# A PEER decoder block: token groups (0,1,2)+(3) become (0,1)+(2,3), block 0 gathers its U rows and adds its weights to a DRAM table

## The chip, the cores and the metric

The kernel runs on one core of a Trainium2 chip. A time is the device time of one execution in microseconds (us). Engine names are those of the profile: PE is TensorE (PEld its weight loads), DVE is VectorE, ACT is ScalarE, POOL is GpSimd, SP issues most DMAs.

## The reference

One decoder block over 512 tokens of width 1024 plus 16 meta tokens. First a mixer: stick-breaking attention (8 heads of 64) beside gated linear attention (4 heads), one input projection and one output projection. Then the PEER layer, which takes most of the time:

```
q = (t @ w_peer_q)                      # per token 8 heads, two halves of 64
s1, s2 = q1 . sub_keys1, q2 . sub_keys2 # 128 scores each
16 best of each, 16 best of the 256 sums -> 16 experts (of 128*128) and softmax gates per head
act = gelu(expert_u[e] . x)             # 128 experts per token
y   = sum over e of gate * act * expert_v[e]
```

A final RMSNorm follows. Each of `expert_u` and `expert_v` is 16384 x 1024 float32 (64 MB).

## The kernel before

The 512 tokens are four blocks of 128. `GROUPS = ((0,1,2),(3,))`: the mixer (`front`, L229) and then output projection, norm and PEER queries (`mid`, L617) run for blocks 0 to 2 together and then for block 3. Group 0 multiplies in three passes over operands split into a high and a low part (`hilo`, L181: a copy on ACT and a subtraction on DVE; `mm3`, L185), group 1 in native float32. `topk` (L702) finds a block's experts and gates, nearly all of it on DVE.

The PEER layer has two forms. **Dense** (blocks 0 to 2): all 128 sets of 128 experts go through PE. `u_phase` (L907) loads 512 KB of U, splits it and makes 24 matmuls of 384 columns (8 feature tiles, three passes), then Gelu. `v_operands` (L954) loads 512 KB of V, multiplies the Gelu by the table of summed gates and splits both; `v_block` (L977) makes 18 matmuls of 512 columns into six PSUM banks. The table of gates, `Gd` in DRAM, is built by `spread` (L827): per 4 tokens a one-hot `B` on DVE, a weighted one-hot `Am` on POOL, matmuls, a copy, and one 1 MB write per 16 tokens. **Gathered** (block 3, `gathered`, L986): per step one indirect DMA on POOL (`gather`, L805) brings 128 rows of 4 KB, one per token; `u_dot` (L811) or `v_sum` (L822) uses them on DVE. 128 steps for U and 128 for V.

Order: `SCHED` (L42) lists by hand how group 1, the lookups, the spreads and three early U products follow each other; then U runs 23 sets ahead (`LA`), and in the dense loop (L1012) every set issues one U set 23 ahead, one V set, and 2.35 steps of `gathered` (`GRATE`). The framework plans the queue of each engine from this order: what is listed first goes first where its operands are taken to be ready, later work fills the gaps, and `keep_in_program_order` (L813, L824) holds the gathered DVE steps behind all that was listed before them. At run time each engine takes its queue in that order. Waits are derived from what each instruction reads and writes, DRAM tables included.

Of the kernel before, what the change touches and what calls it, by code (L numbers as in the profile page):

```python
# [21 lines left out]
D = 1024  # L22
# [8 lines left out]
GB = 5  # L31
# PSUM banks for the key scores of the four blocks
SCT = ("px", "pz", "pz", "px")
# [4 lines left out]
GRATE = 2.35  # L38
TRATE = 16
# order in which the second group and the dense blocks' lookups are issued: f, m mixer pieces and middle of the second  # L40
# group; c, t key scores and top 16 of a block; s spreading of its weights; u a number of early U products
SCHED = "f f f u1 f f t0 c1 f f f f m s0 t1 c2 s1 u1 u1 t2 s2 m c3"  # L42
LNEXP = "natural_log_exp_and_others"
# pairs (a, b) of two descending lists that can be among the 16 largest sums: (a+1)(b+1) <= 16
# [12 lines left out]
ND = len(DENSE)  # L57
TT = 16
TB = ND * 128 // TT
IC = 8  # L60
# float32 products as four passes (True) or as three passes over operands split in two (False), per token group
NATIVE_IN = (False, True)
NATIVE_OUT = (False, True)
NATIVE_PQ = (False, True)


def build(tc, d, out):
# [14 lines left out]

    wp = pool_open("wts", "wts0", side="right")
# [4 lines left out]
    # PSUM banks: 8 = pj 2, pz 3, po 3 (first group); pj 2, pk 2, pz 2, px 2 (second group); pj 2, acc 6  # L88
    nbuf = dict(pz=3, po=3)

    def pj():
        return psA.tile([128, 512], F32, name="pj", bufs=2)

# [13 lines left out]
    Gd = drp.tile([TB, 128, 128, TT], F32, name="Gd")  # L107
    hd = drp.tile([4, 128, D], F32, name="hd")

# [20 lines left out]
    csel = cp.tile([128, 240], F32, name="csel")  # L130

# [4 lines left out]
    def consts_b():  # L136
        nc.sync.dma_start(wgu, d["wgu"])
        nc.sync.dma_start(bgu, d["bgu"])
        lvf = pp.tile([128, 8, 128], F32, name="kT0")
# [14 lines left out]
        P.memset(csel[:, 112:128], -1.0)  # L154
        V.tensor_copy(cb[:, 0, :], ident)
        V.tensor_copy(cb[:, 1, :], cmf)

# [1 line left out]
    def rstd(ss, n, np_, pool, tag):  # L159
        """(ss / D + eps) ** -0.5 of sums of squares [np_, n]: exp(-ln / 2) and one Newton step."""  # L160
# [68 lines left out]
    def front(g):  # L229
        """Both mixer branches for the query blocks of group g; the meta tokens go with group 0."""  # L230
# [8 lines left out]
        oTh = (pp if g == 0 else wp).tile([128, KT, W], F32 if nato else F32R, name=f"oT{g}h")  # L239
        oTl = None if nato else pp.tile([128, KT, W], F32R, name=f"oT{g}l")  # L240
# [4 lines left out]
        kT = (pp if g == 0 else ap).tile([128, 4, W], F32, name=f"kT{g}")  # L245
        vt = (pp if g == 0 else ap).tile([128, nb, 512], F32, name=f"v{g}")
# [4 lines left out]
        tags = itertools.cycle(("pz", "po"))  # L251

        def norm_rows(x, rows):
            """Rows of x over their root mean square, in place."""
# [6 lines left out]
        def columns(x, rows, col, q):  # L261
            """A quarter of the features of normalised rows as columns of hn."""
# [26 lines left out]
        def rows_(c, vtile, mtile):  # L289
            """A chunk of values: tokens on partitions."""  # L290
            banks, outs, jobs = token_jobs(nb, NM, pm_)
            if g == 0:
                pm = banks[-1][:66, 256:]
                jobs.append((pm, 't', 0, 256, 0, 66, False))
# [25 lines left out]
        def gla_scores():  # L320
# [1 line left out]
            p = pm_()  # L322
            proj(win, 12, [(p[:66, :nt], 'f', 0, 66, c0, E, True)], act, nat, cols=66)
            A.activation(glr[:, c0:], p[:16, :nt], AF.Copy)
            for pr in range(2):
# [14 lines left out]
            for m, p in enumerate(feat(6, NM)):  # L340
                A.activation(gq[:, m], p, AF.Copy, scale=0.125)
            for m, p in enumerate(feat(7, c0)):
                A.activation(gk[:, m, c0:], p, AF.Copy)

# [35 lines left out]
            for l in range(8):  # L380
                level(l)

        def gla_values():
            for c in range(2):
                cs = slice(c * 256, (c + 1) * 256)
                rows_(8 + c, gv[:, :, cs], gvm[:, cs] if g == 0 else None)

        def gla_out():
# [34 lines left out]
            for b, blk in enumerate(blks):  # L423
# [11 lines left out]
                if blk < 3:  # L435
                    state(NM + b * 128, 128, gv[:, b], False)

        def gla_silu():
            for c in range(2):
                for m, p in enumerate(feat(10 + c, NM)):  # L440
# [4 lines left out]
                    V.tensor_tensor(gr[:, 2 * c + m], p, e, op=OP.mult)  # L445

        def gla_norm():
            np_ = 2 if 2 * W <= 512 else 1
            n = np_ * W
            for s in range(2):  # L450
                for pr0 in range(0, 2, np_):
# [7 lines left out]
                    for j in range(np_):  # L459
# [6 lines left out]
                        else:  # L466
                            V.tensor_mul(rr[:, c_], rr[:, c_], gr[:, hh])
                            hilo(oTh[:, 4 + hh], oTl[:, 4 + hh], rr[:, c_])

        def sb_proj():  # L470
# [1 line left out]
            for c in range(2):  # L472
                for m, p in enumerate(feat(c, NM)):
                    A.activation(sbq[:, 2 * c + m], p, AF.Copy, scale=0.125)
            for c in range(2):
                for m, p in enumerate(feat(2 + c, c0)):
                    A.activation(kT[:, 2 * c + m], p[:, NM - c0:], AF.Copy)
                    if g == 0:
                        for s in range(2):
                            A.activation(kbd[s * 64:(s + 1) * 64, 2 * c + m, s * 16:(s + 1) * 16],  # L480
                                         p[s * 64:(s + 1) * 64, :NM], AF.Copy)
            for c in range(2):
                cs = slice(c * 256, (c + 1) * 256)
                vm = pp.tile([NM, 256], F32, name="vm", bufs=2) if g == 0 else None
                rows_(4 + c, vt[:, :, cs], vm)
                if g == 0:
# [6 lines left out]
        def sb_attn():  # L493
# [12 lines left out]
            pO.extend([po(), po(), po()] if g == 0 else [pk()])  # L506
# [3 lines left out]
            for kg, kb in tiles:  # L510
# [4 lines left out]
                for pr0 in range(0, 4, nh):  # L515
                    for s in range(2):
# [29 lines left out]
                        for i in range(nh):  # L546
                            pr = pr0 + i
                            hh = 2 * pr + s
                            for b in range(q0 // 128, nb):
# [3 lines left out]
                                         start=(own and b == kb and pr == 0), stop=False, skip_group_check=True)  # L553
            z = pz()[:, :W]
# [17 lines left out]
        def sb_norm():  # L572
            for b in range(nb):
# [11 lines left out]
                if not nato:  # L585
                    hilo(oTh[:, :4, ob], oTl[:, :4, ob], rr.rearrange("p (a t) -> p a t", a=4))

        for piece in ORDER[g]:
            if piece == "n":
# [15 lines left out]
                if g == 0:  # L605
                    consts_b()
            else:
                dict(l=gla_scores, v=gla_values, o=gla_out, r=gla_silu, x=gla_norm, q=sb_proj, a=sb_attn, y=sb_norm)[piece]()
            if piece != ORDER[g][-1]:
                yield  # L610
        es.close()
        yield

    xns = {}
    pers = {}

    def mid(g):  # L617
        """Output projection, residual, second norm, PEER queries of a group."""
# [3 lines left out]
        nato, natq = NATIVE_OUT[g], NATIVE_PQ[g]  # L622
        pm_ = pj if g == 0 else pk
        oTh, oTl = oTs[g]
        hp_ = tc.tile_pool(name=f"h{g}", bufs=1, side="right", reuse_waits="tile")
# [8 lines left out]
        if g == 0:  # L634
            # both halves of the contraction for all columns: the first only needs the attention heads
            two = [pj(), pj(), po(), po()]
            one = [po(), pz()]
# [485 lines left out]
```

## Time and profile before

| | before |
|---|---|
| median of 2 runs | 1711.76 us (1710.41 to 1713.12) |
| span of the profiled execution (the page gives no other time of it) | 1712.3 us |
| PE / DVE / ACT / POOL busy | 1625.8 / 1230.3 / 703.9 / 529.2 us |
| DMA moved | 376.04 MB, mean 220 GB/s |

Busy time is what an engine's instructions took; a busy PE includes pipelined matmuls that overlap, so what it really delivers is read from the distance between the starts of two matmuls. The kernel has three parts in time: group 0 (to about 334 us), group 1 with lookups, spreads and the first U sets (to 732 us, the first V matmul), and the dense loop (to 1697 us).

### The profile page before, as it was taken

How to read it: one execution, taken by the hardware profiler on the slowest of the kernel's cores; microseconds unless marked ns; L12 is line 12 of the kernel's file. 1: busy time of each engine (PE TensorE's matmuls, PEld its weight loads, DVE VectorE, ACT ScalarE, POOL GpSimd, SP SyncE). 2: the span in 40 equal slices, each digit the busy share in tenths (PEclk: the TensorE clock that was granted, in tenths of full speed). 3: DMA queues.
4: the chain of work that ended last, by engine and by line, in shares of the span. 5: the costliest groups of instructions: out<-in, count | busy, mean ns of one | idle time of the engine just before them, and what ended most of it. 6: DMA issues, size and time to landing. Idle time of an engine off the chain costs nothing.

```text
span 1712.3 us, 24535 instructions
## 1 busy us (share of the span) xinstructions
PE 1625.8 (95%) x9025; PEld 1448.6 (85%) x9025; DVE 1230.3 (72%) x2484; ACT 703.9 (41%) x1104; POOL 529.2 (31%) x401
## 2 busy tenths in 40 slices
PE   6999998988888799999999999999999999999996
PEld 5967988976678788989999999999999999999885
DVE  4225737389989998988777777777777777777674
ACT  5357355324455566333333333333333333333343
POOL 0020000002455565045434344343344443434310
PEclk9989999999999899999999999999999999999998
DMA  5210215243254345689887887887888887877653
GB/s 173 82 38 28 96 63 191 82 153 111 99 195 187 136 177 214 201 271 375 322 301 280 301 320 281 315 299 277 309 304 295 303 302 293 307 278 281 213 200 134
DMA packets 145705, 376.04 MB, mean 220 GB/s; under 512 B 13712, under 2 KB 63008, under 8 KB 142512
## 3 DMA queue, kind: packets, MB, share of 16 engines
q1 hardware_dynamic: 104112, 211.92, 36.2%
q0 software_dynamic: 36864, 134.23, 21.2%
q10 hardware_dynamic: 4608, 28.31, 4.1%
q8 instruction: 71, 1.16, 0.3%
q14 instruction: 50, 0.41, 0.1%
HBM read 345.03 MB, written 29.36 MB: 219 GB/s over the span
## 4 chain that ended last, share of the span: by engine, by line
PE 77%; DVE 14%; DMA 4%; ACT 2%; issue 1%; POOL 1%; SPq 0%; DVEq 0%; ACTq 0%; POOLq 0%
PE pj L189 12%; PE pj L187 12%; PE pj L188 12%; PE acc L188 9%; PE acc L189 9%; PE acc L187 9%; PE pk L209 3%; DVE B L859 2%; PE px L865 2%; PE pz L522 1%; PE pz L373 1%; PE pz L530 1%; DVE sc L775 1%; DMA gu<-expert_u,idx 1%; DMA vf<-expert_v 1%
## 5 line engine op out<-in xcount | busy, mean ns | idle before, releaser
L189 PE MATMUL pj<-xDh,ul 128*128 128x384 f32 x1000 | 337.3, 337 | 2.5 <-DVE ul L183 2.5
L187 PE MATMUL pj<-xDh,uh 128*128 128x384 f32 x1000 | 336.6, 337 | 0.0
L188 PE MATMUL pj<-xDl,uh 128*128 128x384 f32 x1000 | 336.2, 336 | 0.0
L188 PE MATMUL acc<-vl,wh 128*128 128x512 f32 x762 | 298.8, 392 | 2.8 <-DVE vl L183 2.8
L189 PE MATMUL acc<-vh,wl 128*128 128x512 f32 x762 | 298.6, 392 | 0.0
L187 PE MATMUL acc<-vh,wh 128*128 128x512 f32 x762 | 296.2, 389 | 0.0
L807 POOL DMA_INDIRECT gu<-expert_u,idx x128 | 189.4, 1479 | 324.2 <-DVE gu L814 183.7
L807 POOL DMA_INDIRECT gu<-expert_v,idx x128 | 178.7, 1396 | 277.2 <-DVE y L825 201.5
L182 ACT ACTIVATE uh<-uf 128x1024 fp32r<-128x1024 f32 x125 | 132.5, 1060 | 304.0 <-PE pj L188 262.4
L183 DVE TENSOR_TENSOR ul<-uf,uh 128x1024 fp32r<-128x1024 f32 x125 | 157.3, 1258 | 56.1 <-ACT uh L182 56.1
L187 PEld LDWEIGHTS pj<-xDh,uh 128*128 128x128 f32 x1000 | 188.3, 188 | 4.2
L188 PEld LDWEIGHTS pj<-xDl,uh 128*128 128x128 f32 x1000 | 188.2, 188 | 4.0
L189 PEld LDWEIGHTS pj<-xDh,ul 128*128 128x128 f32 x1000 | 188.2, 188 | 3.9 <-DVE ul L183 3.5
L188 PEld LDWEIGHTS acc<-vl,wh 128*128 128x128 f32 x762 | 143.0, 188 | 32.2 <-DVE vl L183 4.3
L189 PEld LDWEIGHTS acc<-vh,wl 128*128 128x128 f32 x762 | 143.0, 188 | 29.8
L187 PEld LDWEIGHTS acc<-vh,wh 128*128 128x128 f32 x762 | 143.1, 188 | 27.8 <-ACT vh L182 0.4
L825 DVE SCALAR_TENSOR_TENSOR y<-gu,act,y 128x1024 f32<-128x1024 f32 x128 | 163.9, 1280 | 0.5
L183 DVE TENSOR_TENSOR vl<-vf,vh 128x1024 fp32r<-128x1024 f32 x127 | 155.1, 1221 | 10.2 <-ACT vh L182 10.2
L861 POOL TENSOR_TENSOR Am<-ohu,ohl 128x512 f32<-128x512 f32 x96 | 132.6, 1399 | 95.3 <-PE px L865 57.8
L814 DVE SCALAR_TENSOR_TENSOR gu<-gu,xn 128x1024 f32<-128x1024 f32 x128 | 154.7, 1219 | 8.1 <-DMA gu<-expert_u,idx 8.1
L182 ACT ACTIVATE vh<-vf 128x1024 fp32r<-128x1024 f32 x127 | 133.0, 1047 | 16.7 <-DMA vf<-expert_v 14.4
L865 PE MATMUL px<-Am,B 128*128 128x128 f32 x768 | 105.5, 289 | 24.8 <-DVE B L859 13.2
(365 smaller groups left out, 2507.9 us busy)
## 6 DMA issues: line engine op xcount, KB each, us to landing
vf<-expert_v SPq DMA_DIRECT2D x128, 512.0 KB, 3.7
uf<-expert_ut SPq DMA_DIRECT2D x125, 512.0 KB, 5.0
wf<-w_in SPq DMA_DIRECT2D x48, 512.0 KB, 3.7
Gd<-st ACTq DMA_DIRECT2D x24, 1024.0 KB, 4.0
gt<-Gd SPq DMA_DIRECT2D x16, 1536.0 KB, 12.4
wf<-w_out SPq DMA_DIRECT2D x16, 512.0 KB, 3.7
wf<-w_pq SPq DMA_DIRECT2D x16, 512.0 KB, 3.7
h<-x SPq DMA_DIRECT2D x4, 512.0 KB, 6.5
```

The source lines that it names most:

```text
L182: A.activation(hi, src, AF.Copy)
L183: V.tensor_tensor(lo, src, hi.bitcast(F32), op=OP.subtract)
L187: T.matmul(outp, lh, rh, start=first, stop=False, skip_group_check=True)
L188: T.matmul(outp, lh, rl, start=False, stop=False, skip_group_check=True)
L189: T.matmul(outp, ll, rh, start=False, stop=last, skip_group_check=True)
L209: T.matmul(o, l, r, start=st, stop=sp, skip_group_check=True)
L807: P.indirect_dma_start(out=u, out_offset=None, in_=d[table], in_offset=bass.IndirectOffsetOnAxis(ap=col, axis=0))
L814: V.scalar_tensor_tensor(u, u, 1.0, xns[blk], op0=OP.mult, op1=OP.mult, accum_out=acts[blk][:, k:k + 1]))
L825: V.scalar_tensor_tensor(y, u, acts[blk][:, k:k + 1], y, op0=OP.mult, op1=OP.add))
L859: V.tensor_tensor(B, io4, iT[:, 1, c_].unsqueeze(2).to_broadcast(sh), op=OP.is_equal)
L861: P.tensor_tensor(Am.rearrange("p t (u l) -> p t u l", l=8), ohu[:, l_].unsqueeze(3).to_broadcast([128, 4, 16, 8]), ohl[:, l_].unsqueeze(2 ...
L865: T.matmul(p[:, j * 128:(j + 1) * 128], B[:, j], Am[:, j], start=True, stop=True)
```

## The change

Groups are (0,1) and (2,3). Block 0 (`HALF`) gathers U rows (128 steps) but takes part in the dense V sums; block 1 (`FULL`) gathers U and V; blocks 2 and 3 (`DENSE`) are dense in both. So dense U matmuls have 256 columns instead of 384, dense V still covers three blocks (0, 2, 3). Gather steps are 384 instead of 256; spreads are two instead of three. Block 0's finished weights (gate times Gelu) go into a second DRAM table `Gs`, zeroed at the start by 16 DMAs of 512 KB on ACT's queue, by 128 indirect DMAs on POOL that add single float32 words (one per token and step); the dense loop reads `Gs` beside `Gd` and splits it. Each step's scatter comes 32 steps after its gather. The layout of `Gd` is turned: writes of 512 B pieces, reads of 8 KB pieces. The PEER queries are native float32 in both groups. U and V are handled in pairs of sets; U runs 18 pairs ahead. Instead of the hand-written order, generators yield a planned cost and `weave` mixes background steps into them at fixed rates.

```diff
-GB = 5
+GB = 6
-GROUPS = ((0, 1, 2), (3,))
-DENSE = (0, 1, 2)
-GATHER = (3,)
+GROUPS = ((0, 1), (2, 3))
+DENSE = (2, 3)
+HALF = 0
+FULL = 1
+VBLK = (HALF,) + DENSE
+RATES = (0.72, 1.0, 0.5)
+LA = 18
...
-    Gd = drp.tile([TB, 128, 128, TT], F32, name="Gd")
+    Gd = drp.tile([NK // IC, 128, TB, IC * TT], F32, name="Gd")
+    Gs = drp.tile([NK // IC, 128, IC * 128], F32, name="Gs")
...
+        P.memset(zer, 0.0)
+        for i in range(NK // IC):
+            nc.scalar.dma_start(Gs[i].rearrange("p (a x) -> p a x", a=2), zer.unsqueeze(1).to_broadcast([128, 2, 512]))
...
+        if blk == HALF:
+            fp = fp.rearrange("p h k -> p (h k)")
...
+            V.scalar_tensor_tensor(places, se[:, 1], 1024.0, cs, op0=OP.mult, op1=OP.add)
...
+    flat = Gs.rearrange("g p x -> (g p x)").unsqueeze(1)
+
+    def scatter(blk, k):
+        P.indirect_dma_start(out=flat, out_offset=bass.IndirectOffsetOnAxis(ap=places[:, k:k + 1], axis=0),
+                             in_=acts[blk][:, k:k + 1], in_offset=None, compute_op=OP.add)
+
+    def half(blk):
+        n = NK // 4
+        for k in range(NK + n):
+            if k < NK:
+                u_dot(blk, k)
+            if k >= n:
+                scatter(blk, k - n)
+            if k < NK and k % n == n - 1:
+                weights(blk, slice(k - n + 1, k + 1))
+            yield 1.3 if k < n else 2.8
+
+    def gathered(blk):
+        for k in range(NK):
+            u_dot(blk, k)
+            yield 1.3
+        weights(blk, slice(0, NK))
+        y = gb.tile([128, D], F32, name=f"y{blk}")
...
+        for k in range(NK):
+            v_sum(blk, y, k)
+            yield 1.3
...
+    def weave(main, rate):
+        for cost in main:
+            owed[0] += cost * rate
+            while owed[0] > 0:
+                c = background()
...
+    rows.append(half(HALF))
+    rows.append(tks[1])
+    weave(f1, RATES[0])
+    weave(mid(1), RATES[0])
+    finish(rows)
...
+    look.extend([tks[2], tks[3], spread(DENSE[0], 3), spread(DENSE[1], 3)])
+    weave(ahead(LA), RATES[1])
+    finish(look)
...
+    def dense():
+        for p_ in range(NPAIR):
+            if p_ + LA < NPAIR:
+                u_pair(p_ + LA)
+            ops = v_operands(p_)
...
+            yield 13.8 if p_ + LA < NPAIR else 8.2
+
+    rows.append(gathered(FULL))
+    weave(dense(), RATES[2])
+    finish(rows)
```

## Rows read from the trace of the kernel before

**Rows 1.** The page: busy time, share of the span and instructions of each engine.
```profile
PE 1625.8 (95%) x9025; PEld 1448.6 (85%) x9025; DVE 1230.3 (72%) x2484; ACT 703.9 (41%) x1104; POOL 529.2 (31%) x401
```

**Rows 2.** The page: the chain that ended last, by engine.
```profile
PE 77%; DVE 14%; DMA 4%; ACT 2%; issue 1%; POOL 1%; SPq 0%; DVEq 0%; ACTq 0%; POOLq 0%
```

**Rows 3.** Stretches: length, PE, PEld, DVE, ACT, POOL busy; clock, DMA share, GB/s.
```profile
82.00:166.00 84.00, 84.00 (x389) 55.77 (x388) 28.61 (x51) 52.77 (x102) 15.11 (x26) 0.94 0.07 26
166.00:246.00 80.00, 79.19 (x597) 70.32 (x596) 45.77 (x84) 31.19 (x55) 0.31 (x1) 1.00 0.23 80
246.00:300.00 54.00, 48.06 (x357) 44.90 (x357) 37.99 (x70) 33.56 (x72) 0.31 (x1) 0.94 0.50 171
300.00:334.00 34.00, 34.00 (x201) 34.00 (x200) 9.43 (x13) 12.07 (x21) 0.00 (x0) 1.00 0.17 62
334.00:732.00 398.00, 351.25 (x2274) 312.76 (x2273) 363.85 (x1275) 191.88 (x280) 142.71 (x104) 0.96 0.46 163
732.00:1697.00 965.00, 962.25 (x4797) 866.44 (x4796) 707.91 (x903) 345.61 (x487) 368.05 (x256) 1.00 0.81 288
1697.00:1712.00 15.00, 1.31 (x6) 0.75 (x4) 7.40 (x22) 2.15 (x8) 0.00 (x0) 0.70 0.42 140
```

**Rows 4.** One line's forms: V matmuls, count, duration, first and last start.
```profile
L187 PE MATMUL acc<-vh,wh x762: 387/389/497, 732.1 to 1696.8; 128*128 128x512 f32 x191
```

**Rows 5.** PE in time: start, duration; 17 V matmuls, then U.
```profile
1099.67 0.40 PE L188 MATMUL acc<-vl,wh 128*128 128x512 f32 x1
...
1103.56 0.33 PE L187 MATMUL pj<-xDh,uh 128*128 128x384 f32 x1
...
1104.44 0.34 PE L189 MATMUL pj<-xDh,ul 128*128 128x384 f32 x1
```

**Rows 6.** PE in time in group 0: fourteen matmuls of 256 columns.
```profile
64.88 0.28 PE L187 MATMUL pj<-wh,hnh 128*128 128x256 f32 x1
...
66.42 0.27 PE L188 MATMUL pj<-wl,hnh 128*128 128x256 f32 x1
```

**Rows 7.** Groups of instructions: count, busy us, mean ns, idle before and releaser.
```profile
L807 POOL DMA_INDIRECT gu<-expert_u,idx x128 | 189.4, 1479 | 324.2 <-DVE gu L814 183.7 <-DVE gate L801 70.3 <-DVE y L825 59.2
L814 DVE SCALAR_TENSOR_TENSOR gu<-gu,xn 128x1024 f32<-128x1024 f32 x128 | 154.7, 1219 | 8.1 <-DMA gu<-expert_u,idx 8.1
L183 DVE TENSOR_TENSOR vl<-vf,vh 128x1024 fp32r<-128x1024 f32 x127 | 155.1, 1221 | 10.2 <-ACT vh L182 10.2
L861 POOL TENSOR_TENSOR Am<-ohu,ohl 128x512 f32<-128x512 f32 x96 | 132.6, 1399 | 95.3 <-PE px L865 57.8 <-DVE ohl L853 22.3 <-issue 10.7
L859 DVE TENSOR_TENSOR B<-io,iT 128x512 f32<-128x512 f32 x96 | 90.3, 952 | 4.4 <-PE px L865 4.1
L848 DVE TENSOR_TENSOR ohu<-io,iT 128x256 f32<-128x256 f32 x24 | 19.5, 814 | 5.9 <-POOL Am L861 5.9
L732 DVE FIND_INDEX8 iu<-vv,sc 128x8 uint32<-128x128 f32 x64 | 17.1, 282 | 0.0
L775 DVE SCALAR_TENSOR_TENSOR sc<-bb,fi 128x128 f32<-128x128 f32 x64 | 17.2, 340 | 0.0
L779 DVE TENSOR_REDUCE cs<-sc 128x128 f32<-128x2048 f32 x4 | 15.0, 3739 | 0.0
L751 DVE FIND_INDEX8 pu<-tv,cand 128x8 uint32<-128x50 f32 x32 | 5.9, 204 | 0.0
```

**Rows 8.** DMA issues: what, queue, count, KB each, median us to landing.
```profile
vf<-expert_v SPq DMA_DIRECT2D x128, 512.0 KB, 3.7
gu<-expert_u,idx POOLq DMA_INDIRECT x128, 6.2
vbd<-vm SPq DMA_DIRECT2D x8, 4.0 KB, 1.7
```

**Rows 9.** Stretches as in rows 3: the fastest transfers, and the steady dense loop.
```profile
745.00:800.00 55.00, 53.42 (x273) 48.56 (x272) 44.05 (x68) 18.53 (x26) 28.88 (x19) 1.00 1.05 371
800.00:1000.00 200.00, 200.00 (x1014) 182.13 (x1013) 148.62 (x192) 70.71 (x100) 81.24 (x57) 1.00 0.85 304
```

More of the change, by code (lines that the diff above doesn't have):

```diff
@@ L130, in build @@
     csel = cp.tile([128, 240], F32, name="csel")
+    zer = cp.tile([128, 512], F32, name="zer")
+    row = cp.tile([128, 1], F32, name="row")
     def consts_a():
@@ L867, in spread, with step, background, finish @@
                              p.rearrange("p (t i) -> p t i", t=4), AF.Copy)
-            nc.scalar.dma_start(Gd[128 // TT * DENSE.index(blk) + tb], st)
+                yield 1.0
+            nc.scalar.dma_start(Gd[:, :, 128 // TT * DENSE.index(blk) + tb].rearrange("g p x -> p g x"),
+                                st.rearrange("p (g l) t -> p g (l t)", l=IC))
+    ys = {}
+    flat = Gs.rearrange("g p x -> (g p x)").unsqueeze(1)
[15 more added lines that the diff above has]
+            u_dot(blk, k)
+            yield 1.3
+        weights(blk, slice(0, NK))
+        y = gb.tile([128, D], F32, name=f"y{blk}")
+        ys[blk] = y
+        nc.sync.dma_start(y, hd[blk])
+        for k in range(NK):
+            v_sum(blk, y, k)
+            yield 1.3
+    look, rows = [], []
+    def step(queue):
+        while queue:
+            c = next(queue[0], None)
+            if c is not None:
+                return c
+            queue.pop(0)
+        return None
+    mixed = [0.0]
+    def background():
+        if look and (not rows or mixed[0] < 1.0):
+            c = step(look)
+            if c is not None:
+                mixed[0] += MIX
+                return c
+        mixed[0] -= 1.0
+        return step(rows)
+    owed = [0.0]
+    def weave(main, rate):
[3 more added lines that the diff above has]
+                c = background()
+                if c is None:
+                    owed[0] = 0.0
+                    break
+                owed[0] -= c
+    def finish(queue):
+        while step(queue) is not None:
+            pass
     for _ in front(0):
@@ new lines, in build @@
+    gb = ctx.enter_context(tc.tile_pool(name="gat", bufs=1, reuse_waits="tile"))
+    wp = pool_open("wts", "wts1", side="right")
+    ps = pool_open("ps", "psb1", space=PSUM)
+    f1 = front(1)
+    next(f1)
+    for _ in range(1000):
+        if next(tks[0], None) is None:
+            break
+    rows.append(half(HALF))
[3 more added lines that the diff above has]
+    finish(rows)
+    pool_close("wts")
+    pool_close("kv")
+    pool_close("ps")
+    nbuf["px"] = 6
@@ L915, in u_phase, with u_pair @@
+    ps = pool_open("ps", "psb2", space=PSUM)
+    bp = pool_open("bld", "bld", side="right")
+    du = ctx.enter_context(tc.tile_pool(name="dnu", bufs=1, reuse_waits="tile"))
+    ring = {}
+    def u_pair(p_):
+        ge = ring[p_] = du.tile([128, 2, DT], F32, name="ge", bufs=LA + 1)
+        pu = pj()
+        for i in range(2):
             uf = du.tile([128, KT, 128], F32, name="uf", bufs=2)
@@ new lines, in u_pair, with ahead @@
+            hilo(uh, ul, uf)
+            for kt in range(KT):
+                mm3(pu[:, i * DT:(i + 1) * DT], (uh[:, kt], ul[:, kt]), (xDh[:, kt], xDl[:, kt]), kt == 0 and i == 0,
+                    kt == KT - 1)
+        A.activation(ge.rearrange("p a t -> p (a t)"), pu, AF.Gelu)
+    def ahead(n):
+        for p_ in range(n):
+            u_pair(p_)
+            yield 5.6
+    look.extend([tks[2], tks[3], spread(DENSE[0], 3), spread(DENSE[1], 3)])
+    weave(ahead(LA), RATES[1])
+    finish(look)
@@ L1032, in build, with v_pair @@
-    for _ in gen:
-        pass
-    for i in range(ND):
-        for j in range(2):
-            for i1 in sorted(last):
-                v_block(i1, i, last[i1], (j,))
+            hilo(vh, vl, vf)
+            hl.append((vh, vl))
+        return (wh, wl), hl
+    def v_pair(p_, ops, ijs):
+        (wh, wl), vs = ops
+        for e in range(2):
+            first, last = p_ == 0 and e == 0, p_ == NPAIR - 1 and e == 1
+            for i, j in ijs:
+                ts, ds_ = slice(i * 128, (i + 1) * 128), slice(j * 512, (j + 1) * 512)
+                mm3(acc[i][j], (wh[:, e, ts], wl[:, e, ts]), (vs[e][0][:, ds_], vs[e][1][:, ds_]), first, last)
```

330 lines of the change are left out of this document (120 added, 210 removed).

## The prediction

> **What bounds the kernel now.** I read the engines' totals first: PE is busy for 1625.8 of 1712.3 us, DVE 1230.3, POOL 529.2 [rows 1], and PE holds 77% of the chain that ended last, DVE 14% [rows 2]. Then I cut the span where the work changes [rows 3]. Up to 334 us group 0 runs on PE with few pauses. From 334 to 732 us PE (351 of 398) and DVE (364, so 91%) are both nearly full: lookups, spreads and group 1 on DVE, projections and the first U sets on PE. From 732 us, where the first V matmul starts [rows 4], to 1697 PE never pauses (962 of 965) while DVE has a quarter free. So the dense loop is bound by PE, the stretch before it by PE and DVE together, and the last 15 us are the final norm.
>
> What PE delivers is the distance of starts. 17 V matmuls of 512 columns take 1103.56 - 1099.67 = 3.89 us, 0.229 us each; five U matmuls of 384 columns 0.88 us, about 0.174 each [rows 5]. A set is 24 x 0.174 + 18 x 0.229 = 8.3 us. Check: 732 + 105 sets x 8.3 + the 23 whose U ran ahead x 4.12 = 1698, against 1697 in the rows.
>
> The profiled span, 1712.3 us, lies within the two runs (1710.41 to 1713.12), so the sum is made in span time and carried to the median unchanged.
>
> **The change part by part.**
>
> *Dense U, 256 columns.* Matmuls of that width with the same loads start every (66.42 - 64.88)/13 = 0.118 us in group 0 [rows 6]. A pair of sets is 48 x 0.118 = 5.7 us of U and 36 x 0.229 = 8.24 us of V: 13.9 us, where before two sets took 16.6. This is the gain: 128 x 24 x (0.174 - 0.118) = 172 us of PE.
>
> *Group 0 with two blocks instead of three.* 82 to 166 us is attention: six block pairs become three and score steps go from 14 to 6, 84 to about 47. 166 to 246 shrinks with its columns, 80 to 58; 246 to 300 from 54 to 42; the PEER queries lose their splits but take four passes, 34 to 30 [rows 3]. The 82 us before that become 63: a weight chunk cannot go faster than load, split and two buffers allow, (3.7 + about 2.3)/2 = 3 us, the 3.7 being a 512 KB load [rows 8]. Sum 240. The 16 zeroing DMAs (8.4 MB, 23 us at 371 GB/s [rows 9]) compete with the first weight loads; nothing at best, 20 at worst, I take 5: **245 us**.
>
> *Before the first V matmul, DVE.* A lookup: five rows like the 17.1 us one make 79 us for four blocks, two like 17.2 make 31, two like 15.0 make 30, five like 5.9 some 26 [rows 7]; with small copies 172 us for four. 128 U steps of block 0: 1.22 plus the read of the sum, 160. Two spreads instead of three: (90.3 + 19.5 + 24 for two smaller one-hots) x 2/3 = 89. Splits of 36 U sets at 1.2: 43. The DVE work of group 1's mixer: what 364 us leaves after lookups, three spreads and U splits is some 40 for one block, 75 for two. Sum 539; at the 91% of rows 3, 590 us. From 245 that gives **835**. PE has less: 351 now, about 70 more for a second block in native float32, some 40 more for attention and for 36 sets of U at 2.85 instead of 23 at 4.15, a spread less, so under 460, hidden beside DVE. The extra ACT work (703.9 of 1712 busy) is hidden too.
>
> *Before the first V matmul, POOL.* The new operation is the adding scatter, and no row shows one. All of them write the same table, so each must wait until the one before has landed; the wait stands in POOL's queue, and behind it stand the next gather, `Am` of the spreads and the small additions of attention. The first V operands need the table, hence the last scatter. One step costs P. Lower end: two POOL instructions of 1.48 without any wait, 2.96 [rows 7]. Upper end: a scatter lands as late as a 512 KB gather, 6.2 [rows 8]. In between: a transfer of 512 KB lands in 3.7 and one of 4 KB in 1.7, so the data is 2.0, and a small transfer on the gathers' path would land in 6.2 - 2.0 = 4.2; the last 32 have no gather ahead of them, so I take **4.0**. The lookup of block 0 (about 50 us of DVE) ends near 295, 32 gathers without scatters end at 342, and 128 x 4.0 leads to **855**. Reading and adding the word in DRAM is not in this number; it can only raise it.
>
> The Trainium skill ("DMA: Bandwidth & Descriptors", Rules for kernel authors) says that an accumulating DMA must wait for the semaphore of an earlier one on the same bytes; no row here shows one, and it speaks against this change. The same page (Anatomy of one DMA) gives about 2.0 us fixed per DMA of this path: as an estimate by it P would be 3.48, POOL would end at 787, and DVE's 835 would stand, for a total of 1654.
>
> *First V matmul:* the later chain, **855**, against 732 now. This is the price of the change: 123 us.
>
> *The dense loop.* 46 pairs carry U, 18 only V. Per pair DVE has now 148.6/(200/8.27) = 6.1 us per set [rows 9], of it 2.35 gather steps at 1.25; the rest for a pair is 6.4, and 6.9/1.3 = 5.3 steps add 6.6: 13.0 of 13.9 us, tight but under PE. POOL 5.3 x 1.48 = 7.8. DMA: four loads and 5.3 gathers of 512 KB and 0.39 MB of tables are 5.27 MB, 379 GB/s at PE's pace; the best stretch of the trace moved 371 [rows 9], so 14.2 us a pair. The upper end is the 304 GB/s of the steady loop, 17.3, but there PE, not DMA, set the pace (share 0.85), so I take the nearer row. 46 x 14.2 = 653, 18 x 8.24 = 148. Gathers end by pair 48, before the loop does.
>
> The Trainium skill (same page, Bandwidth) gives about 358 GB/s from HBM per core; by it a pair would take 14.7 and the total rise by 23. The row of 371 GB/s disagrees with it.
>
> *End:* 15 us as now and 3 for the first operands. **Sum:** 855 + 653 + 148 + 18 = 1674, 2.2% under 1712.
>
> **The rivals.** (1) *The scatter chain decides, slower.* The place is the wait of scatter k on scatter k-1 in POOL's queue. The total meets today's when the first V matmul starts at 893, so at P = (893 - 342)/128 = 4.3. With P = 5, 342 + 640 = 982 and the total is 1801; with 6.2, 1136 and 1955. For it: gathers stand in front of it and the word is read, added and written. Against: 128 words are little, and the stretch before V is half empty on DMA (share 0.46 [rows 3]). Chance 0.27.
>
> (2) *Transfers bound the dense loop.* At 330 GB/s a pair takes 16.0 and the total is 1757; at 304, 17.3 and 1817. For it: DMA's share is already 0.85 [rows 9]. Against: the 512 B reads of the table go away. Chance 0.13.
>
> (3) *DVE idles behind the gathers.* The U steps are pinned in DVE's order. If nothing fills the 4.0 - 1.25 us between them, the last ends at 342 + 96 x 4.0 = 726 and three lookups (129), spreads (89) and splits (43) follow: 987, total 1806; half filled, 920 and 1739. Chance 0.10.
>
> (4) *The change does not do what I take it to do:* scatters are not chained, P = 2.96, POOL ends at 721, DVE's 835 stands: 1654. Chance 0.05.
>
> **How the numbers follow.** My forecast, 1674, has 0.45. Two per cent, about what a measurement of this kernel can tell from no change, is 34 us: faster means under 1678, slower over 1746. The forecast's own range is 1620 (DVE packed to 95%, 812, and pairs at PE's 13.9) to 1710; 0.38 of it counts as faster, 0.07 as same. Rival 1 gives 0.21 slower and 0.06 same, rival 2 0.05 and 0.08, rival 3 0.05 and 0.05, rival 4 0.04 faster and 0.01 same. Faster 0.42, same 0.27, slower 0.31. The range reaches from 1620 to rival 1 at P = 5, 1802; beyond lie its worst cases and a faster end than DVE allows, under 0.2.
>
> **What would show it.** Right: U matmuls of 256 columns 0.118 us apart; the first V matmul near 855, with DVE over 85% busy before it; scatters on POOL about 4 us apart; a pair of 14 to 14.5 us with PE over 95% busy. Wrong: scatters 5 us apart or more and PE idle until the table is done (rival 1); PE pauses in the dense loop released by `vf`, `uf` or `gu` transfers (rival 2); DVE waiting for gathers with lookups behind them (rival 3); scatters 3 us apart (rival 4).

## The result, and the profile after

The changed kernel takes **1946.6 us** (median; 1945.07 to 1948.09), the kernel before 1711.8: a ratio of 1.137, 95% interval 1.132 to 1.143. It is slower, by 235 us; the forecast was 1674, with 1620 to 1802 as its range.

First the page: the engines' busy time and the chain that ended last.

```profile
PE 1534.6 (79%) x8618; PEld 1313.2 (68%) x8618; DVE 1312.2 (68%) x2575; ACT 712.7 (37%) x1018; POOL 860.0 (44%) x621
...
PE 47%; DMA 18%; issue 16%; POOL 9%; DVE 6%; ACT 3%; ACTq 1%; POOLq 0%; SPq 0%; DVEq 0%
```

PE does 91 us less than before [rows 1], as a narrower U wants, but it no longer holds the chain: 47% instead of 77% [rows 2]. Stretches of the same execution (length, PE, PEld, DVE, ACT, POOL busy; clock, DMA share, GB/s):

```profile
272.00:318.00 46.00, 13.84 (x82) 9.45 (x80) 44.61 (x266) 10.88 (x33) 0.00 (x0) 0.66 0.16 52
318.00:413.00 95.00, 81.38 (x378) 65.20 (x378) 70.36 (x169) 19.79 (x43) 43.89 (x36) 0.82 0.75 265
413.00:705.00 292.00, 204.48 (x769) 141.84 (x769) 123.94 (x357) 127.53 (x170) 154.52 (x114) 0.83 0.48 139
705.00:930.00 225.00, 121.28 (x874) 116.60 (x873) 178.93 (x627) 55.76 (x69) 139.00 (x94) 0.77 0.68 202
930.00:1148.00 218.00, 116.45 (x727) 108.76 (x726) 130.82 (x145) 78.94 (x84) 137.44 (x101) 0.73 0.46 120
1148.00:1774.00 626.00, 620.94 (x3680) 554.72 (x3680) 567.62 (x696) 244.53 (x309) 361.89 (x240) 0.99 0.99 381
1774.00:1929.00 155.00, 155.00 (x685) 128.02 (x684) 85.82 (x105) 61.60 (x90) 13.30 (x10) 1.00 0.51 174
```

The cuts are: the queries of group 0 end at 272, the lookup of block 0 at 318, the first 32 U steps at 413; the queries of group 1 end at 705, the last two lookups at 930; the first V matmul starts at 1148, U ends at 1774 and V at 1929. One line's forms (count, duration, first and last start) give the start of V, in the row that answers to [rows 4]:

```profile
L208 PE MATMUL acc<-vh,wh x768: 387/389/720, 1147.8 to 1928.7; 128*128 128x512 f32 x192
```

The same view of the queries' line gives the end of group 1's queries:

```profile
L230 PE MATMUL pk<-xT,wf x128: 379/379/792, 671.5 to 705.2; 128*128 128x256 f32 x128
```

**1148 instead of 855, and the whole miss lies here.** From 1148 on the kernel runs a little faster than forecast: 46 pairs in 626 us (13.6 each) with PE 99% busy, 18 pairs in 155, 14 at the end; 795 where the sum had 819. Ahead of it no engine is the bound: from 318 to 1148 DVE is busy for 504 of 830 us, PE for 524, POOL for 475.

What POOL does from the first scatter to the last (its groups, count | busy us, mean ns | idle before and releasers):

```profile
L909 POOL DMA_INDIRECT Gs<-act,places x128 | 228.1, 1782 | 189.6 <-DMA Gs<-act,places 167.9 <-issue 10.9 <-DVE act L848 6.2
L836 POOL DMA_INDIRECT gu<-expert_u,idx x98 | 110.4, 1126 | 78.0 <-DVE gu L843 52.1 <-issue 22.3 <-DVE ul L204 0.9
L892 POOL TENSOR_TENSOR Am<-ohu,ohl 128x512 f32<-128x512 f32 x45 | 59.9, 1570 | 3.3 <-PE px L896 2.8 <-DVE ohl L883 0.3 <-POOL Am L892 0.2
L576 POOL TENSOR_TENSOR RS<-RS,sp 128x512 f32<-128x512 f32 (+1 forms) x12 | 13.0, 1083 | 6.7 <-PE pz L565 5.2 <-PE pz L568 1.2
```

A scatter with its wait is (228.1 + 189.6)/128 = 3.26 us; where nothing else stands between two of them POOL in time (start, duration, idle before and releaser) shows the same:

```profile
953.00 1.55 POOL L909 DMA_INDIRECT Gs<-act,places  x1 [1.71 <-DMA Gs<-act,places]
956.41 1.55 POOL L909 DMA_INDIRECT Gs<-act,places  x1 [1.86 <-DMA Gs<-act,places]
```

The 128 steps take 1089 - 414 = 675 us, 5.3 each: besides the 3.26 there are gathers, 52 us of waiting for DVE to free their buffers, 60 us of `Am` and the sums of attention. The last scatter is not yet the end: of the 59 us from it to 1148 the chain that ended last spends most in the spreads (`B`, `Am` and their products), which stand between and behind the scatters on POOL, and the rest in the last write of `Gd` and its reading back (start, duration):

```profile
1131.47 6.46 DMA Gd<-st
1137.99 5.54 DMA gt<-Gd
```

### The profile page after: what moved, and what is told of

Its sections match the earlier page's. It is cut to its first block, busy times and chain, and to the rows that moved or that the text cites. A ratio compares the mean times of both kernels' runs of the same rounds, so it can differ in the third digit from the quotient of the medians.

```text
span 1943.1 us, 23969 instructions
## 1 busy us (share of the span) xinstructions
PE 1534.6 (79%) x8618; PEld 1313.2 (68%) x8618; DVE 1312.2 (68%) x2575; ACT 712.7 (37%) x1018; POOL 860.0 (44%) x621
## 4 chain that ended last, share of the span: by engine, by line
PE 47%; DMA 18%; issue 16%; POOL 9%; DVE 6%; ACT 3%; ACTq 1%; POOLq 0%; SPq 0%; DVEq 0%
DMA Gs<-act,places 11%; PE acc L208 7%; PE acc L209 7%; PE acc L210 7%; POOL gu L836 5%; PE pj L210 5%; PE pj L208 5%; PE pj L209 5%; POOL Gs L909 3%; DMA gu<-expert_u,idx 2%; PE pk L230 2%; DVE B L890 2%; PE px L896 1%; DMA wf<-w_in 1%; DMA wf<-w_out 1%
## 5 line engine op out<-in xcount | busy, mean ns | idle before, releaser
L836 POOL DMA_INDIRECT gu<-expert_u,idx x256 | 345.7, 1350 | 436.4 <-DVE gu L843 200.5
L210 PE MATMUL pj<-xDh,ul 128*128 128x256 f32 x1024 | 302.9, 296 | 115.4 <-DVE ul L204 111.5
L843 DVE SCALAR_TENSOR_TENSOR gu<-gu,xn 128x1024 f32<-128x1024 f32 x256 | 307.2, 1233 | 99.2 <-DMA gu<-expert_u,idx 98.3
L208 PE MATMUL pj<-xDh,uh 128*128 128x256 f32 x1024 | 300.1, 293 | 17.4 <-ACT ge L1024 16.4
L909 POOL DMA_INDIRECT Gs<-act,places x128 | 228.1, 1782 | 189.6 <-DMA Gs<-act,places 167.9
L209 PE MATMUL pj<-xDl,uh 128*128 128x256 f32 x1024 | 298.9, 292 | 0.0
L210 PEld LDWEIGHTS pj<-xDh,ul 128*128 128x128 f32 x1024 | 206.1, 201 | 120.6 <-DVE ul L204 116.1
L208 PEld LDWEIGHTS pj<-xDh,uh 128*128 128x128 f32 x1024 | 206.6, 202 | 19.6 <-ACT ge L1024 16.5
L209 PEld LDWEIGHTS pj<-xDl,uh 128*128 128x128 f32 x1024 | 206.0, 201 | 1.7
L896 PE MATMUL px<-Am,B 128*128 128x128 f32 x512 | 85.8, 332 | 74.2 <-POOL Am L892 58.7
```

What stands on the lines that cost most here:

```text
L208: T.matmul(outp, lh, rh, start=first, stop=False, skip_group_check=True)
L209: T.matmul(outp, lh, rl, start=False, stop=False, skip_group_check=True)
L210: T.matmul(outp, ll, rh, start=False, stop=last, skip_group_check=True)
L836: P.indirect_dma_start(out=u, out_offset=None, in_=d[table], in_offset=bass.IndirectOffsetOnAxis(ap=col, axis=0))
L843: V.scalar_tensor_tensor(u, u, 1.0, xns[blk], op0=OP.mult, op1=OP.mult, accum_out=acts[blk][:, k:k + 1]))
L896: T.matmul(p[:, j * 128:(j + 1) * 128], B[:, j], Am[:, j], start=True, stop=True)
```

## The experiments

Two theories stood first: (A) the scatters' chain on POOL makes the 293 us; (B) they come from DVE's work, which cannot be packed as forecast. All times are medians beside runs of the kernel before on the same chip (1713 to 1716); F is the start of the first V matmul, Q the end of group 1's queries, both read in the profiled execution.

**Scatters left out** (the function does nothing).
```diff
-        P.indirect_dma_start(out=flat, ..., compute_op=OP.add)
+        pass
```


> Leaves out the 128 adding scatters, so block 0's share of the PEER sum stays zero; all else as in the changed kernel. Theory A (the chain of scatters, 675 us from the first to the last, sets the first V matmul): it moves from 1148 us to 880-960, where DVE's work ends, total 1680-1760. Rival B (the U steps, pinned in DVE's order, hold up lookups and spreads whatever POOL does): the first V matmul stays past 1050, total over 1850. In both the part from the first V matmul on stays at about 795 us.


1825.8 us, F 1028, Q 702: neither. The scatters cost 121 us; 173 of the 293 stand without them. Its stretches:

```profile
272.00:318.00 46.00, 14.53 (x75) 9.89 (x74) 45.23 (x268) 11.38 (x33) 0.00 (x0) 0.64 0.16 51
318.00:413.00 95.00, 77.40 (x386) 61.88 (x385) 75.77 (x187) 25.60 (x52) 49.55 (x41) 0.88 0.79 288
413.00:702.00 289.00, 204.26 (x759) 140.63 (x758) 133.66 (x366) 121.02 (x159) 91.24 (x78) 0.83 0.47 160
702.00:871.00 169.00, 118.21 (x852) 111.52 (x851) 157.56 (x597) 55.40 (x68) 45.80 (x34) 0.85 0.63 222
871.00:1027.00 156.00, 105.08 (x745) 99.04 (x744) 124.33 (x145) 76.81 (x84) 84.44 (x64) 0.88 0.55 166
```

DVE's column adds up to 537 us, where the forecast had 539. The work was sized right; it takes 755 us instead of 590, since from 413 to 702 DVE is 46% busy.

**A third spread in place of scatters, second table and zeroing.**
```diff
-            if k >= n:
-                scatter(blk, k - n)
...
+    look.extend([tks[2], spread(HALF, 3), tks[3], spread(DENSE[0], 3), spread(DENSE[1], 3)])
```


> Block 0's weights go the way of the dense blocks' gates: a third spread (one-hot products on PE, DVE, POOL) into the same table, no scatter, no second table, no zeroing. Theory A: about 205 us of POOL and the chain go, 45 us of DVE and 45 of POOL come: first V matmul at 900-960, total 1700-1760. Rival B: as the spread of block 0 must follow its 128 U steps, the first V matmul is no earlier than 1050, total over 1850.


1840.0 us, F 1044: neither. That is 107 us less than with the scatters, and 14 more than without scatters and spread. The spread itself costs more than these 14, since the zeroing is gone here too: group 0's queries end at 252 instead of 271.

**The scatter writes instead of adding.**
```diff
-                             in_=acts[blk][:, k:k + 1], in_offset=None, compute_op=OP.add)
+                             in_=acts[blk][:, k:k + 1], in_offset=None)
```


> The scatters write their words instead of adding them, so experts chosen by two heads of a token count once; waits and order are the same. If reading and adding the word in DRAM is what a scatter costs (theory A1), scatters without a gather between them come every 2.3-2.8 us instead of 3.3, and the total falls by 50 us or more. If issue and landing are the cost (theory A2), the distance stays at 3.2-3.4 us and the total within 15 us of 1947.


1888.2 us, F 1092: theory A1, by the total and by the distance. POOL's group of scatters, and two that follow each other with nothing between:

```profile
L909 POOL DMA_INDIRECT Gs<-act,places x128 | 159.2, 1244 | 188.5 <-DMA Gs<-act,places 161.0 <-issue 19.9 <-DVE act L848 4.1
...
928.60 0.96 POOL L909 DMA_INDIRECT Gs<-act,places  x1 [1.43 <-DMA Gs<-act,places]
930.98 0.96 POOL L909 DMA_INDIRECT Gs<-act,places  x1 [1.42 <-DMA Gs<-act,places]
```

The instruction is 0.54 us shorter on average, 69 us over 128. The waits for the scatter before sum to nearly the same, 161 us instead of 168. Where nothing stands between two scatters they come 2.4 us apart instead of 3.3: the instruction takes 0.96 instead of 1.55 us and the wait 1.4 instead of 1.7. So adding makes mostly the instruction dearer, and the landing a little.

**Two tables by turns**, so that a scatter waits for the one before the last (both zeroed during group 0, added when read).
```diff
+    Gss = [drp.tile([NK // IC, 128, IC * 128], F32, name=f"Gs{i}") for i in range(NG)]
...
+        P.indirect_dma_start(out=flats[k % NG], ...)
```


> Two tables take the scatters in turn, so that each waits only for the one before the last; both are zeroed piece by piece during group 0 and added when loaded. The number of scatters and their POOL time stay. Theory A (the wait is the cost): pairs of scatters without gathers at POOL's 1.6-1.9 us each, about 190 of the 675 us of the chain gone, and some 20 us from the later zeroing: total 1720-1790. If POOL's own time for scatters and gathers is the cost (theory C, 860 us busy): the wait gone changes little, total over 1850.


1936.9 us, F 1093, with the wait on the scatter before down from 168 to 32 us: theory C. F gains 55, of which the late zeroing alone is worth 26 (below), so 136 us less of waiting moved F by about 29. The loop behind it, which also loads and adds the second table, takes 49 more.

**Rate of weaving 1.6 instead of 0.72.**
```diff
-RATES = (0.72, 1.0, 0.5)
+RATES = (1.6, 1.0, 0.5)
```


> The changed kernel with one number altered: block 0's gather-and-scatter steps and block 1's lookup are woven into group 1's mixer at a rate of 1.6 instead of 0.72, so that all of them stand before the end of the mixer in the written order. Theory A (the dense blocks belong to group 1, and their lookups and spreads must follow its PEER queries, so DVE has too little that it may do before about 705 us): the first V matmul stays between 1120 and 1170, the total between 1920 and 1970. Rival B (the work is there, but the written order puts block 0's U steps and scatters behind the mixer): the U steps all end before 705 instead of near 850, the first V matmul comes before 1080 and the total is under 1880.


1900.6 us, F 1105, Q 758: between the two. Block 0's steps come earlier (last scatter 969), and the mixer of group 1 ends 53 us later.

**Block 0's U steps left out as well.**
```diff
-    rows.append(half(HALF))
```


> Leaves out block 0's U gathers, U dot products and scatters (block 0's expert sum then is not the reference's). What is left before the first V matmul is group 0, its lookups, group 1's mixer, and the dense blocks' lookups and spreads. Theory A (a serial chain: group 1's mixer has its own length, then lookups, then spreads): against 1028 for the version without scatters only the U steps that ran after 702 us go (41 us of DVE in 702 to 800): PEER queries of group 1 end between 660 and 705, the first V matmul comes at 940 to 1000, total 1735 to 1790. Rival B (the pinned U steps in DVE's and POOL's queues hold the mixer up): the queries end before 620, the first V matmul before 900, total under 1690.


1686.0 us, F 882, Q 610. The rival B of this run held: 128 U steps with 156 us of DVE moved F by 145, though DVE had, without them, this hole (443 to 612):

```profile
443.00:612.00 169.00, 138.23 (x590) 95.97 (x592) 24.25 (x47) 50.95 (x93) 15.86 (x18) 0.90 0.19 66
```

One reason why the hole did not take them is seen on ACT, in time, in one attention step: the changed kernel first, then this one.

```profile
490.65 0.60 ACT L531 ACTIVATE az<-pz 128x512 f32<-128x512 f32 x1 [1.05 <-PE pz L556]
491.27 1.28 ACT L533 ACT_TABLE_LOAD   x1
492.56 0.63 ACT L533 ACTIVATE az<-az 128x512 f32<-128x512 f32 x1
493.21 1.28 ACT L532 ACT_TABLE_LOAD   x1
494.50 0.63 ACT L532 ACTIVATE az<-az 128x512 f32<-128x512 f32 x1
495.15 1.28 ACT L533 ACT_TABLE_LOAD   x1
```
```profile
469.89 0.60 ACT L531 ACTIVATE az<-pz 128x512 f32<-128x512 f32 x1 [0.32 <-PE pz L556]
470.38 0.62 ACT L533 ACTIVATE az<-az 128x512 f32<-128x512 f32 x1
470.90 0.62 ACT L532 ACTIVATE az<-az 128x512 f32<-128x512 f32 x1
471.55 0.63 ACT L533 ACTIVATE az<-az 128x512 f32<-128x512 f32 x1
```

Block 0's first Gelu runs at 412.9, inside group 1's mixer, and takes the joint table of exp and ln off ACT; from then to 705 each exp and ln that follows the other reloads its own, 48 loads in all, 62 us of ACT. Attention steps are 7.1 us apart instead of 5.1.

**Tables kept**: the joint table is loaded again behind each of block 0's four Gelus; in the changed kernel, without scatters, and with the third spread.
```diff
         i = A.activation(a, a, AF.Gelu)
+        tc.keep_in_program_order(i)
+        if blk == HALF:
+            tc.keep_in_program_order(A.preload_act_table_set(LNEXP))
```


> The changed kernel with one instruction more: behind each of block 0's four Gelu activations the joint table of exp and ln is loaded again on ACT. In the changed kernel the first of these Gelus falls into group 1's mixer, and from then on each softplus step of the attention reloads tables (about 45 loads of 1.28 us before the queries; 7.1 us from step to step, against 5.1 in the version without block 0's steps). Theory A (these loads are on group 1's chain): attention steps 5.1 to 5.5 us apart, the queries of group 1 end at 645 to 675 instead of 705, the total falls by 30 to 60 us to 1885 to 1915. Rival B (ACT has room, and the scatters on POOL or DVE's work set the end anyway): total 1935 to 1955.

> The same instruction added to the version that leaves out the scatters (block 0's sum is then missing). Theory A: queries at 645 to 670 instead of 702, first V matmul at 970 to 995 instead of 1028, total 1765 to 1790. Rival B (the U steps pinned in DVE's order, not the tables, make the mixer longer by 92 us than it is without them): queries after 690, total over 1810.

> The same instruction added to the version in which block 0's weights go through a third spread, without scatters, second table or zeroing. Theory A: queries at 640 to 670 instead of 702, first V at 985 to 1010 instead of 1044, total 1780 to 1805, still above the kernel before. Rival B: total over 1825.


1915.2, 1778.7 and 1803.7 us: 31, 47 and 36 less. Q comes at 672, 655 and 662, F at 1121, 978 and 1002. Theory A held in all three. In the first the total is at the edge of its range, and the attention steps are 5.9 us apart, more than expected.

**Zeroing spread over group 0's mixer.**
```diff
     for _ in front(0):
-        pass
+        if i < 16:
+            nc.scalar.dma_start(Gs[i % 16]...)
```


> The changed kernel with its 16 zeroing transfers issued one at a time between the pieces of group 0's mixer instead of all at the start. Theory A (they delay group 0's first weights by about 20 us, and all behind it hangs on that in series): the queries of group 0 end at 250 to 256 instead of 271, the first V matmul comes 15 to 25 us earlier, total 1920 to 1932. Rival B (what sets the first V matmul takes it up, or the transfers collide with later weight loads): total within 1938 to 1955.


1920.0 us, F 1122, group 0's queries at 254 instead of 271: theory A, at the edge of its range. In the changed kernel ACT's own queue shows why the zeroing weighs so much; eleven issues hold ACT for 14 us while group 0's first weight splits wait behind them (the last row, of ACT):

```profile
24.14 13.81 ACTq L175 DMA_DIRECT2D Gs<-zer  x11
38.00 2.00 ACT L203 ACTIVATE wh<-wf 128x1024 fp32r<-128x1024 f32 x2 [14.73 <-DMA Gs<-zer]
```

**Dense blocks 1 and 2**, block 3 gathering both tables, and the spreads of blocks 0 and 1 in the mixer's second half (rate 1.45, four gather buffers); with block 3's lookup in the dense loop, and ahead of it.
```diff
-DENSE = (2, 3)
+DENSE = (1, 2)
...
-RATES = (0.72, 1.0, 0.5)
+RATES = (1.45, 1.0, 0.5)
...
+                rowq.extend([spread(0, 2), spread(1, 2)])
```


> Dense blocks 1 and 2 instead of 2 and 3, block 3 gathers both tables, block 0's weights go through a third spread and no scatter; the spreads of blocks 0 and 1 stand in the second half of group 1's mixer (rate 1.45), block 3's lookup in the dense loop; for room 4 gather buffers instead of 6 and 11 pairs of U ahead instead of 18. Theory A (what is late are the lookups and spreads of dense blocks that belong to group 1; only one lookup and one spread are left behind the queries): first V matmul at 850 to 920, then 53 pairs of 13.6, 11 of 8.3 and 14: total 1675 to 1745. Rival B (the mixer of group 1 cannot take the spreads beside it, it gets longer by what they cost): queries of group 1 end after 770, first V after 960, total over 1785.

> As the version with the spreads of blocks 0 and 1 in group 1's mixer and dense blocks 1 and 2, but with block 3's lookup ahead of the dense loop and 18 pairs of U ahead. Theory A: one more lookup (about 43 us of DVE, up to 60 in time) behind the queries: first V matmul at 900 to 980, then 781 and 14: total 1695 to 1775. Rival B (the mixer is lengthened by the spreads): first V after 1010, total over 1805.


1872.9 and 1886.1 us, F 989 and 1040, Q 823 and 832. Rival B held, by its numbers: with the third spread behind the queries Q was 702, and here it is some 120 us later. That is not shown to be the spreads alone, which take 156 us for two when they stand alone (871 to 1027 above): the rate rose as well, and 1.6 alone moved Q by 53. Both versions still reload the tables.

**Lookups of blocks 2 and 3 on group 0's queries**, without scatters, tables kept, rate 1.6.
```diff
-RATES = (0.72, 1.0, 0.5)
+RATES = (1.6, 1.0, 0.5)
...
-        qp = qps[g]
+        b = blk % 2
+        qp = qps[0]
...
+    rows.extend([tks[1], tks[2], tks[3]])
```


> The version without scatters and with the tables kept (1779, first V 978), but the lookups of blocks 2 and 3 read group 0's queries in place of their own (so the dense blocks' experts are not the reference's) and may run as soon as DVE has room, woven at rate 1.6; every instruction is as before in number and size. Theory A (what is left over the forecast is the wait of the dense blocks' lookups for group 1's queries, with DVE idle in group 1's mixer): lookups end by 720, first V matmul at 860 to 910, total 1650 to 1705. Rival B (the mixer cannot take lookups beside it, and becomes longer by as much): queries of group 1 end after 725 instead of 655, first V after 945, total over 1745.


1733.3 us, F 927, Q 706: between. The lookups end 87 us earlier than with their own queries (739 against 826), the mixer 51 us later, F comes 51 earlier. But the rate has its part in all of this: in the changed kernel 1.6 alone put Q 53 us later and F 43 earlier. The run shows that the lookups end earlier when they need not wait; what that wait is worth by itself it does not show.

**All U gathers ahead of all scatters.**
```diff
-            if k >= n:
-                scatter(blk, k - n)
...
+        for k in range(NK):
+            scatter(blk, k)
+            yield 1.5
```


> The changed kernel with all 128 U gathers of block 0 ahead of its 128 scatters, so that no gather stands between two scatters. Theory A (a scatter alone takes what it took where nothing stood between two of them, 1.55 us of POOL and 1.75 of waiting, 3.3 us; the 5.3 us per step came from what stands between): scatters 3.2 to 3.6 us apart, except behind spreads' Am; U steps end by about 790, scatters by 1210 to 1260, total 2010 to 2080. Rival B (adding words into one table takes 5 us or more by itself): scatters 5 to 5.5 us apart, ending after 1420, total over 2240.


1977.7 us. The group of scatters sums to (222.7 + 230.4)/128 = 3.5 us each, so theory A on the size. They still run from 559 to 1187: the written order did not keep them together, other work of POOL came between. Their end and the total lie below theory A's ranges.

**Three amendments together**: tables kept, late zeroing, rate 1.6.


> The changed kernel with three amendments that gained alone: tables of exp and ln loaded again behind block 0's Gelus (1915 alone), zeroing spread over group 0's mixer (1920 alone), rate 1.6 instead of 0.72 (1901 alone). Theory A (the three lie one behind the other in one chain): the gains of 31, 27 and 46 us add up: first V matmul near 1045, total 1835 to 1865. Rival B (behind them all the chain of 128 scatters on POOL sets the end): first V not before 1085, total 1880 to 1900.


1896.9 us, F 1098: rival B. The gains (31, 27, 46) do not add up; the last scatter is at 967 and F 131 us behind it. Two stretches show what stands there:

```profile
855.00:967.00 112.00, 17.32 (x88) 15.92 (x87) 19.67 (x26) 9.25 (x11) 60.58 (x41) 0.55 0.18 21
967.00:1097.00 130.00, 86.18 (x620) 80.13 (x621) 104.08 (x119) 68.06 (x73) 76.24 (x58) 0.88 0.58 175
```

The lookups are done at 855, but the spreads need `Am` from POOL, and that stands behind the scatters: DVE does 20 us in 112, and 104 in the 130 behind.

**`Am` on DVE**, in the last version and in the one with the third spread and kept tables.
```diff
-                P.tensor_tensor(Am.rearrange("p t (u l) -> p t u l", l=8),
+                V.tensor_tensor(Am.rearrange("p t (u l) -> p t u l", l=8),
```


> The version with the three amendments (1897, scatters end at 967, spreads' Am products on POOL run from 949 to 1078, DVE busy 20 of 112 us between 855 and 967), with the Am products on DVE instead of POOL. Theory A (the spreads stand in POOL's queue behind the scatters, so the two come one after the other): scatters end near 945 to 970 and the spreads run beside them; first V matmul at 965 to 1010, total 1760 to 1805. Rival B (the spreads are late for another reason, or DVE pays for Am what POOL paid): first V after 1060, total over 1855.

> The version with a third spread instead of scatters and with the tables kept (1804), with Am on DVE. Here nothing stands in POOL's queue ahead of Am. Theory A (only scatters made Am late; DVE is the fuller engine behind group 1's queries): no gain, 1795 to 1835. Rival B (B and Am hinder each other between DVE and POOL, 1.55 us for B instead of 0.69, so that one engine alone is as quick or quicker): 1765 to 1790.


1865.5 us, F 1064: 31 less, and by the numbers rival B, though not by its reasons. The spreads do now run early, from 864 to 959 (DVE 106 of 112); it is the scatters that end at 1054 instead of 967 (the last section shows why). Without scatters 1771.7 us, 32 less, rival B: `B` and `Am` hinder each other. Their groups, with `Am` on POOL and then on DVE:

```profile
L877 POOL TENSOR_TENSOR Am<-ohu,ohl 128x512 f32<-128x512 f32 x96 | 133.7, 1415 | 204.4 <-DVE ohl L868 142.7 <-PE px L881 52.3 <-issue 8.7
...
L875 DVE TENSOR_TENSOR B<-io,iT 128x512 f32<-128x512 f32 x96 | 108.9, 1160 | 16.1 <-PE px L881 16.1
```
```profile
L875 DVE TENSOR_TENSOR B<-io,iT 128x512 f32<-128x512 f32 x96 | 65.4, 682 | 8.8 <-PE px L881 8.8
...
L877 DVE TENSOR_TENSOR Am<-ohu,ohl 128x512 f32<-128x512 f32 x96 | 64.1, 681 | 0.0
```

No version that does the whole work beats the kernel before; the best is this last one, 3.4% over it (interval 2.5 to 4.2%).

## Why the prediction was wrong

**Right.** U matmuls of 256 columns start about 0.12 us apart; the dense loop and the end are 24 us shorter than forecast. Rival 2 did not come about: 381 GB/s over 626 us with PE 99% busy. The Trainium skill ("DMA: Bandwidth & Descriptors", Bandwidth) lets about 358 GB/s bind between HBM and SBUF, which this stretch exceeds; the same section gives 358 as a core's part with both cores of a pair streaming, and this kernel uses one core.

**Wrong: "at the 91% of rows 3, 590 us".** The 539 us of DVE were measured as 537; the 91% was not a property of the stretch but of what stood in it [rows 3]. Before, the lookups and spreads of three dense blocks could run beside the mixer of one block. After, both dense blocks belong to group 1, and their work may start only behind its queries. The version without block 0's U steps shows how much that is. The stretch from group 0's queries to F, in the changed kernel and in that version:

```profile
272.00:1148.00 876.00, 537.42 (x2823) 441.85 (x2822) 548.66 (x1562) 292.91 (x395) 474.85 (x344) 0.78 0.54 159
269.00:882.00 613.00, 481.43 (x2805) 399.56 (x2805) 384.90 (x1300) 226.08 (x339) 108.63 (x88) 0.90 0.35 117
```

DVE's work is 385 us there, near the 379 that the forecast has without the 160 of the U steps; packed to 91% from 245 on, as an estimate, it would end near 660. F came at 882, with DVE 63% busy: 272 us of lookups and spreads stand behind Q, one after the other. What can run beside the mixer, block 0's U steps, makes it longer: by 92 us in the version without scatters (Q 702 against 610), 47 of them the tables. That version reached 71%.

**Mis-sized: PE, "under 460".** The first line above has 537 us for it, the second 481, for about the same number of matmuls. The granted clock averages 0.78 and 0.90 there. What its lower level costs (1.2 instead of 2.4 GHz) the queries' matmuls of the changed kernel show: from 671.5 on, at clock 0.50, five start 0.45 us apart; from 689.9 on, at 1.00, 32 take 7.1 us, 0.22 each. The clock was 0.66 from 272 to 318, where PE was busy for 14 of 46 us, and 0.99 from 1148 to 1774, where it was busy for 621 of 626. How much of PE's longer time lies on the chain was not tried.

**Wrong: "The extra ACT work is hidden".** Counted by busy time it would be. But an early Gelu in a mixer of exp and ln costs 48 table loads on the chain: 31 us of the total, 47 once no scatters lie behind. The kernel before has 9 loads in all, the changed one 58.

**Mis-sized: the zeroing**, 5 forecast, 17 at group 0's queries and 27 in all; the row of the changed kernel shows ACT's instruction stream waiting on the issues, which a bandwidth estimate leaves out.

**Wrong: POOL's chain, 855.** It starts at 414 instead of 342, since block 0's lookup ended at 318 instead of 295 and the first 32 U steps took 95 us instead of 47, while DVE worked for group 1 and block 1's lookup in between. Of the 128 x 4.0 = 512 us, a scatter with its wait is 3.26 and a gather 1.13, 4.4 together and near the guess (the 3.48 that stands beside it in the prediction is near a scatter alone, with no gather in it); the rest of the 675 is `Am`, attention's sums and buffers that DVE frees late. The prediction named `Am` as standing behind the scatters, and gave it no price; it left the adding of the word out, which is 0.9 of a scatter's 3.3 us (2.4 where it writes); and it let the first V matmul start at the last scatter, where 59 us of spreads and of the table `Gd` came behind. The direction is rival 1's: its threshold of 4.3 was passed, and at 5.3 its sum gives 342 + 678 = 1020 and 1839. Yet leaving the scatters out gains only 121 us (137 with the tables kept), and rival 1 alone does not explain 1028 without them. Rival 3's sign, DVE waiting for gathers, showed itself too, but from 413 to 705 as the smaller part behind attention's steps on ACT (waited for: us in total, times, longest):

```profile
DVE sp L534 <- ACT az L533: 61.5, 8, 10.9
DVE gu L843 <- DMA gu<-expert_u,idx: 27.3, 7, 11.2
```

Neither rival had both.

**What stays open.** The parts overlap and do not sum to 293. In the version without scatters and with kept tables F is 978. The run with group 0's queries took 51 us off that, but by the earlier lookups and the higher rate together. How the 96 us that the U steps still cost there (978 against 882) divide between DVE's order, POOL's, the weights' loads and PE's clock was not separated.

## What to carry to other kernels

A share of busy time cannot be carried over a regrouping: ask first which work may run beside which, and whether its inputs exist by then. For every operation moved into another stage, list each queue and each piece of engine state it passes: the ACT tables, the instructions behind its waits, and the buffers it holds. And try the amendments of a slow change together, since behind the first wait stands the next.

## What the runs showed of the hardware

A scatter issued from POOL can last as long as DVE runs two-input operations without a pause. With `Am` on DVE, POOL in time, and then DVE at the end of the second long scatter (start, duration, idle before):

```profile
877.02 37.40 POOL L910 DMA_INDIRECT Gs<-act,places  x1 [1.86 <-DMA Gs<-act,places]
919.83 2.08 POOL L910 DMA_INDIRECT Gs<-act,places  x1 [5.41 <-DMA Gs<-act,places]
923.61 39.13 POOL L910 DMA_INDIRECT Gs<-act,places  x1 [1.70 <-DMA Gs<-act,places]
...
958.95 2.35 DVE L202 TENSOR_TENSOR ul<-uf,uh 128x1024 fp32r<-128x1024 f32 x2
965.04 1.23 DVE L202 TENSOR_TENSOR ul<-uf,uh 128x1024 fp32r<-128x1024 f32 x1 [3.74 <-ACT uh L201]
```

From 877 to 914 DVE was busy for 37.00 of 37 us, 34 of them with `B` and `Am`, and the next scatter starts 42.8 us later; the long one ended at 914.4, when DVE had one-input copies among its work again. During the second long scatter DVE had two-input operations alone; they stopped at 961.3, and the scatter ended at 962.7. These two make most of the 87 us by which the scatters end later in that version. The Trainium skill ("SBUF — State Buffer", Who interferes with whom) states that a DVE instruction with two SBUF inputs contends with a GpSimd instruction that reads SBUF, and these rows agree: the scatter's places and values lie in SBUF. The same section infers that such an operation leaves the writing of descriptors alone; that did not spare these scatters. Which of their accesses was held up was not tried.
